# Gated linear attention of an encoder block: gates computed feature-major for two chunks at once, with a scan on VectorE, and element-wise work taken from GpSimd outside the feed-forward

## The chip, the cores and the metric

The kernel runs on one core of a Trainium2 chip. The core's engines each work through their own instructions in order and meet at semaphores: TensorE (PE for matmuls, PEld for loading weights), VectorE (DVE), ScalarE (ACT), GpSimd (POOL), and SyncE (SP), which here issues every DMA. The metric is device time in microseconds (us) for one execution.

## The reference, cut to what matters

One layer, 1024 tokens, width 1024, float32. Each large matrix product is made of three: both operands are split into a rounded high part and a low remainder, and high·high, high·low and low·high are added up.

```python
h = rms_norm(x, norm_mix_g)
proj = h @ w_in              # gla q,k,v,r, gate codes, swa q,k,v, branch gates
# branch A, 4 heads (dk 128, dv 256), forwards and backwards:
z  = lr @ up + bias
lg = maximum(log_sigmoid(z) / 16, -0.5)          # one log gate per token and feature
b  = cumsum(lg, over the tokens of a chunk)
q_dec, k_inv = q * exp(b), k * exp(-b)
scores = where(mask, q_dec @ k_inv.T, 0)
o = scores @ v + q_dec @ state                   # state: decayed from chunk to chunk
y_gla = (rms_norm(o_fwd + o_bwd, out_g) * silu(r)) @ w_o_gla
# branch B: attention in a window of +-128 tokens, QK norm, rotary positions, sinks
y_swa = windowed_attention(...) @ w_o_swa
x = x + (sigmoid(gate_a) * y_gla + sigmoid(gate_b) * y_swa) @ w_out
x = x + (silu(h2 @ w_gate) * (h2 @ w_up)) @ w_ffn_out,   h2 = rms_norm(x, norm_ffn_g)
```

The products of the feed-forward are done with a seven-product scheme on 2x2 blocks, which this change does not touch.

## The kernel before, in words

**Stages.** In order of time: x is loaded and split and the first projections are made (0 to 55 us); linear attention (GLA, 55 to 470 us); windowed attention (SWA, to about 800 us); the two branch projections and the output projection (to 1100 us); the feed-forward.

**Order of the work.** TensorE's order is written by hand. During GLA and SWA the rest of the input projection runs in between: `dense` is a list of generators (`proj_t`, `proj_f`) that give one 512-column matmul at a time, `fill(n)` takes n of them, and `slot(stages, n)` runs the stages of one slot and spreads n dense matmuls between them. `need(key)` takes more of them until a projection is there. The other engines' orders are settled when the program is built, from priorities and estimated readiness, and are fixed from then on.

**GLA.** Chunks of 128 tokens: 4 heads `hd` of 8 chunks `c`, numbered n = 8·hd + c. The table `at` gives each step its slot: `g_gates` in slot n, `g_sums` in n + 1, `g_scores` in n + 2, `g_out` in n + 3. After a head's eight chunks come the backward states and outputs (`g_back_out`) and `g_turn`, which transposes the finished output and writes it to DRAM. A slot carries 40, 31 or 18 dense matmuls (slots 0 to 5, 6 to 34, and the rest).

- `g_gates` (L324) loads q and k feature-major from DRAM (tile `qk`), makes z token-major with one matmul (gate codes `lrS` stationary, `upS` moving), takes Exp, a clamp and Ln, and splits the result into `lh` and `ll`.
- `g_sums` (L345) makes the cumulative sums b on TensorE: two matmuls a direction, `lh` and `ll` against the triangular constant `U`. Out of PSUM come the chunk sums `sm` and exp(b), exp(-b); multiplied by q and k they are the tiles `eb` and `en`, split into `q2` and `kh`, `kl`. Both low parts are made on GpSimd (L366, L368).
- `g_scores` (L370) splits v (`vl` on GpSimd, L379), transposes `en` into `kth`, `ktl` and makes the scores; `g_out` (L398) makes chunk states `pf`, `kb` and outputs `ob`.

**Weight units.** `wunit` (L62) loads 128x512 weights (tile `wr`), rounds them on ScalarE (`wh`) and takes the remainder `wl` on GpSimd (L68), on VectorE only where a call names it. The dense work draws its units through `next_unit`, which keeps up to three ready (AHEAD = 2); one unit feeds 12 (`proj_t`) or 24 (`proj_f`) matmuls.

**SWA.** `k_prep` and `a_prep` normalise and rotate keys and queries; some of the products are on GpSimd (L513 to L516, L537, L538, L557, L577, L579). `k_turn` (L560) transposes the keys. The first two slots carry 60 dense matmuls each, the next ones 46.

**Buffers.** [...] A `mm` tile is free again when ScalarE (`proj_t`, L210) or VectorE (`proj_f`, L146 and L149) has written it to the staging tile `st`.

Of the kernel before, what the change touches and what calls it, by code (L numbers as in the profile page):

```python
# [8 lines left out]
F32 = mybir.dt.float32  # L9
# [20 lines left out]
def body(tc, i, out):  # L30
    nc = tc.nc
    with ExitStack() as root:
# [29 lines left out]
        def wunit(src, n=512, e=None):  # L62
            raw = wp.tile([P, n], F32, tag="wr", name=nm("wr"), bufs=4)
            nc.sync.dma_start(out=raw, in_=src)
            h = wp.tile([P, n], FR, tag="wh", name=nm("wh"), bufs=5)
            nc.scalar.activation(h, raw, AF.Copy)  # L66
            l = wp.tile([P, n], FR, tag="wl", name=nm("wl"), bufs=5)
            (e or nc.gpsimd).tensor_tensor(l, raw, h.bitcast(F32), op=ALU.subtract)  # L68
            return h, l
# [173 lines left out]
        U = gc.tile([P, 2, P], FR, tag="U", name="U")  # L243
# [28 lines left out]
        with tc.manual_schedule(engines={mybir.EngineType.PE}):  # L272
# [28 lines left out]

            Ur = ip.tile([P, 2, P], F32, tag="Ur", name="Ur")
            nc.sync.dma_start(out=Ur, in_=i["c_u"])
            nc.vector.tensor_scalar(U, Ur, -1.0 / 16, None, op0=ALU.mult)
# [19 lines left out]
        def g_gates(hd, c):  # L324

            a = gla[hd, c] = Chunk()
# [3 lines left out]
            a.qk = gtile("qk", (P, 2, P))  # L330
            nc.sync.dma_start(out=a.qk[:, 0], in_=scr[f"q{hd}", s][:, co:co + P])
            nc.sync.dma_start(out=a.qk[:, 1], in_=scr[f"k{hd}", s][:, co:co + P])
            z = chtile((P, 2, P))
            mm(z, lrS[:, c * P:(c + 1) * P], upS[:, :, hd * P:(hd + 1) * P], True, True)
            e = gtile("e", (P, 2, P), bufs=1)
            nc.scalar.activation(e, z, AF.Exp, scale=-1.0)

            nc.vector.tensor_scalar(e, e, float(np.expm1(8.0)), None, op0=ALU.min)
            nc.scalar.activation(e, e, AF.Ln, bias=ones[:, 0:1])
            a.lh = gtile("lh", (P, 2, P), FR)  # L340
            a.ll = gtile("ll", (P, 2, P), FR)
            nc.vector.tensor_copy(a.lh, e)
            nc.vector.tensor_tensor(a.ll, e, a.lh.bitcast(F32), op=ALU.subtract)

        def g_sums(hd, c):  # L345

            a = gla[hd, c]
            bp = chtile((P, 2, 256))
            for d in range(2):
                mm(bp[:, d], a.lh[:, d], U, True, False)  # L350
                mm(bp[:, d], a.ll[:, d], U, False, True)

            a.sm = gtile("sm", (P, 2, 2), bufs=32)
            nc.vector.tensor_copy(a.sm, bp[:, :, 127:129])
            bc = bp.rearrange("p a (c t) -> p (a c) t", c=2)[:, 0:4:3]
            eb = gtile("eb", (P, 2, P), bufs=1)
            a.en = gtile("en", (P, 2, P))
            nc.scalar.activation(eb, bc, AF.Exp)
            nc.scalar.activation(a.en, bc, AF.Exp, scale=-1.0)
            nc.vector.tensor_tensor(eb, eb, a.qk[:, 0:1].to_broadcast([P, 2, P]), op=ALU.mult)  # L360
            nc.vector.tensor_tensor(a.en, a.en, a.qk[:, 1:2].to_broadcast([P, 2, P]), op=ALU.mult)
            a.q2 = gtile(f"q2{c}", (P, 2, 2, P), FR, bufs=2 if c < 5 else 1)
            a.kh = gtile("kh", (P, 2, P), FR)
            a.kl = gtile("kl", (P, 2, P), FR)
            nc.scalar.activation(a.q2[:, :, 0], eb, AF.Copy)
            nc.gpsimd.tensor_tensor(a.q2[:, :, 1], eb, a.q2[:, :, 0].bitcast(F32), op=ALU.subtract)  # L366
            nc.scalar.activation(a.kh, a.en, AF.Copy)
            nc.gpsimd.tensor_tensor(a.kl, a.en, a.kh.bitcast(F32), op=ALU.subtract)  # L368

        def g_scores(hd, c):  # L370
# [8 lines left out]
            nc.gpsimd.tensor_tensor(a.vl, vr, a.vh.bitcast(F32), op=ALU.subtract)  # L379
            kt = chtile((P, 2, P))  # L380
            for d in range(2):
                nc.tensor.transpose(kt[:, d], a.en[:, d], ident)
# [5 lines left out]
            for d in range(2):  # L388
                mm3(sc[:, d], a.kh[:, d], a.kl[:, d], a.q2[:, d, 0], a.q2[:, d, 1], True, True)
# [8 lines left out]
        def g_out(hd, c):  # L398
# [6 lines left out]
            if c:  # L405
                pf = gla[hd, c - 1].pf
                dec = gtile("dec", (P, 1))
                nc.scalar.activation(dec, a.sm[:, 0, 1:2], AF.Exp, bias=gla[hd, c - 1].sm[:, 0, 0:1])
# [12 lines left out]
            if c:  # L421
                mm3(o, a.q2[:, 0, 0], a.q2[:, 0, 1], th, tl, False, True)
# [3 lines left out]
        def g_back(hd, c):  # L426

            a = gla[hd, c]
            if c < NC - 1:
                n = gla[hd, c + 1]  # L430
                dec = gtile("decb", (P, 1))
                nc.scalar.activation(dec, a.sm[:, 1, 0:1], AF.Exp, bias=n.sm[:, 1, 1:2])
# [8 lines left out]
        def g_back_out(hd, c):  # L441
            a = gla[hd, c]
            if c < NC - 1:
                o2 = chtile((P, 256))
                mm3(o2, a.q2[:, 1, 0], a.q2[:, 1, 1], a.thb, a.tlb, True, True)
# [33 lines left out]
        for n in range(NH * NC):  # L479
            hd, c = divmod(n, NC)  # L480
            cb = hd * NC + NC + 3 + (NC - 1 - c)
            tt = cb + c % 2 + (2 if hd == NH - 1 else 1)
            for j, (t, f) in enumerate(((n, g_gates), (n + 1, g_sums), (n + 2, g_scores), (n + 3, g_out),
                                        (cb, g_back_out), (tt, g_turn))):
                at[t, j + (j == 5 and c % 2)] = (f, hd, c)
# [27 lines left out]
        nc.gpsimd.tensor_tensor(qA[:, :, 0:64], cosb, gb_[0], op=ALU.mult)  # L513
        nc.gpsimd.tensor_tensor(qA[:, :, 64:128], cosb, gb_[1], op=ALU.mult)
# [659 lines left out]
```

## Time and profile before

| | before |
|---|---|
| time, median of 3 runs | 1748.46 us (1748.05 to 1749.23) |
| the profiled execution's own time | 1748.99 us |
| its span in the profile | 1747.2 us |
| busy: PE, PEld | 1701.6, 1408.8 us |
| busy: DVE, ACT, POOL | 1105.4, 866.4, 564.4 us |
| granted TensorE clock, mean | 0.993 |

The busy time of an engine is the time in which at least one of its instructions ran. Matmuls overlap in the pipeline: one of 512 columns takes some 400 ns from start to end, while the next one starts after some 230 ns, so how close TensorE is to its limit is read from the distance between starts. "a<-b,c" names the written and the read tiles without their numbers.

### The profile page before, as it was taken

What the parts mean: (1) busy time and instruction counts of PE and PEld (TensorE: products, weight loads), DVE (VectorE), ACT (ScalarE), POOL (GpSimd) and SP (SyncE); (2) the same over time, 40 slices, a digit from 0 to 9 for tenths busy, and PEclk for the clock granted to TensorE, in tenths of its full rate; (3) what the DMA queues carried; (4) which work ended last, traced back from release to release, by engine and by line L of the source; (5) the groups of instructions that cost most, each with busy time, mean ns of one, the idle gap of its engine ahead of it and who ended that gap; (6) DMA issues with size and microseconds to landing.
All of it is one profiled execution on the core that took longest, in us unless ns stands there. A gap on an engine that the chain in (4) does not pass through costs nothing. (4 is left out here: it accounts for less than half of the span.)

```text
span 1747.2 us, 24463 instructions
## 1 busy us (share of the span) xinstructions
PE 1701.6 (97%) x8008; PEld 1408.8 (81%) x8008; DVE 1105.4 (63%) x1998; ACT 866.4 (50%) x2019; POOL 564.4 (32%) x491
## 2 busy tenths in 40 slices
PE   8999999999999999999999999999999999899998
PEld 6788888888778888878878888788888888787776
DVE  6446666664387655536463268877788888789454
ACT  6455766776447656544454456533333333343342
POOL 3444535544353222112455430333343333100000
PEclk9999999999999999999999999999999999999999
DMA  5433343444533232227766645333234434685333
GB/s 193 138 113 103 119 129 120 122 129 138 167 118 118 88 97 91 79 73 246 238 192 187 193 132 181 109 132 127 91 102 146 152 138 140 233 295 170 96 96 103
DMA packets 158496, 246.03 MB, mean 141 GB/s; under 512 B 18111, under 2 KB 47807, under 8 KB 158369
## 3 DMA queue, kind: packets, MB, share of 16 engines
q1 hardware_dynamic: 158368, 244.48, 43.8%
q8 instruction: 63, 1.03, 0.3%
q14 instruction: 65, 0.52, 0.1%
HBM read 177.30 MB, written 67.11 MB: 140 GB/s over the span
## 5 line engine op out<-in xcount | busy, mean ns | idle before, releaser
L68 POOL TENSOR_TENSOR wl<-wr,wh 128x512 fp32r<-128x512 f32 (+1 forms) x226 | 300.3, 1334 | 471.3 <-ACT wh L66 395.3
L66 ACT ACTIVATE wh<-wr 128x512 fp32r<-128x512 f32 (+1 forms) x256 | 158.1, 625 | 133.7 <-PE mm L72 89.6
L72 PE MATMUL mm<-xh,wh 128*128 128x512 f32 x512 | 205.4, 401 | 6.7 <-ACT xh L263 6.7
L72 PE MATMUL mm<-xl,wh 128*128 128x512 f32 x512 | 205.1, 401 | 0.9 <-DVE xl L264 0.9
L72 PE MATMUL mm<-xh,wl 128*128 128x512 f32 x512 | 172.2, 401 | 0.0
L848 POOL TENSOR_TENSOR ws<-wr,wr 128x512 f32<-128x512 f32 x44 | 67.0, 1525 | 231.3 <-DMA wr<-in_w_fi_dram 126.3
L72 PE MATMUL mm<-wh,xh 128*128 128x512 f32 x320 | 127.0, 397 | 2.6 <-ACT st L210 1.3
L72 PE MATMUL mm<-wh,xl 128*128 128x512 f32 x320 | 126.8, 396 | 0.0
L72 PE MATMUL mm<-wl,xh 128*128 128x512 f32 x320 | 126.3, 395 | 0.0
L72 PEld LDWEIGHTS mm<-xh,wh 128*128 128x128 f32 x512 | 98.0, 191 | 23.3 <-ACT xh L263 6.7
L72 PEld LDWEIGHTS mm<-xl,wh 128*128 128x128 f32 x512 | 97.9, 191 | 18.7 <-DVE xl L264 1.9
L72 PEld LDWEIGHTS mm<-xh,wl 128*128 128x128 f32 x512 | 96.0, 191 | 16.7
L829 ACT ACTIVATE wh<-ws 128x512 fp32r<-128x512 f32 x88 | 55.4, 629 | 98.7 <-PE ch L856 41.5
L829 ACT ACTIVATE wh<-a 128x512 fp32r<-128x512 f32 x66 | 41.7, 632 | 103.2 <-PE mm L992 58.0
L830 DVE TENSOR_TENSOR wl<-ws,wh 128x512 fp32r<-128x512 f32 x88 | 76.4, 875 | 13.5 <-ACT wh L829 13.5
L992 PE MATMUL mm<-hl,wh 128*128 128x512 f32 x176 | 70.7, 402 | 11.0 <-DVE hl L967 11.0
L830 DVE TENSOR_TENSOR wl<-a,wh 128x512 fp32r<-128x512 f32 x66 | 45.5, 691 | 55.1 <-ACT wh L829 55.0
L829 ACT ACTIVATE wh<-wr 128x512 fp32r<-128x512 f32 x52 | 32.9, 632 | 77.9 <-PE ch L856 39.3
L72 PEld LDWEIGHTS mm<-wh,xh 128*128 128x128 f32 x320 | 60.3, 188 | 13.9 <-ACT st L210 2.0
L992 PE MATMUL mm<-hh,wh 128*128 128x512 f32 x176 | 70.0, 398 | 1.2 <-ACT hh L966 1.2
L992 PE MATMUL mm<-hh,wl 128*128 128x512 f32 x176 | 70.1, 398 | 0.0
L72 PEld LDWEIGHTS mm<-wh,xl 128*128 128x128 f32 x320 | 60.3, 188 | 10.0
(502 smaller groups left out, 4785.9 us busy)
## 6 DMA issues: line engine op xcount, KB each, us to landing
wr<-in_w_fi_dram SPq DMA_DIRECT2D x102, 256.0 KB, 2.8
wr<-in_w_t_dram SPq DMA_DIRECT2D x80, 256.0 KB, 2.7
wr<-in_w_f_dram SPq DMA_DIRECT2D x64, 256.0 KB, 2.8
B<-c SPq DMA_DIRECT2D x44, 256.0 KB, 2.1
T<-tx SPq DMA_DIRECT2D x44, 256.0 KB, 2.2
a<-in_w_fo_dram SPq DMA_DIRECT2D x44, 256.0 KB, 4.9
hr<-T SPq DMA_DIRECT2D x44, 256.0 KB, 2.7
hr<-B SPq DMA_DIRECT2D x33, 256.0 KB, 4.0
```

The costliest lines, as they stand in the source:

```text
L66: nc.scalar.activation(h, raw, AF.Copy)
L68: (e or nc.gpsimd).tensor_tensor(l, raw, h.bitcast(F32), op=ALU.subtract)
L72: nc.tensor.matmul(o, a, b, start=start, stop=stop)
L829: nc.scalar.activation(h, src, AF.Copy)
L830: nc.vector.tensor_tensor(l, src, h.bitcast(F32), op=ALU.subtract)
L848: e.tensor_tensor(t, x, y, op=op)
L992: nc.tensor.matmul(ys[m], a[:, c], b, start=f0, stop=f1, skip_group_check=True)
```

## The change: what it does

- **Gates for a pair of chunks, feature-major.** `g_gates` runs for even c only and covers c and c + 1. z is made with `upS` stationary and 256 tokens of `lrS` moving, so features lie on the partitions. The cumulative sum over tokens is a `tensor_tensor_scan` on VectorE (with `mask`, which is 0 at each chunk's first token and 1 elsewhere), so the two matmuls a direction against `U`, the constant `U` and its load, the split into `lh` and `ll`, and the step `g_sums` are gone. Sums, exponentials and products with q and k are done on VectorE and ScalarE on tiles twice as wide. `q2` is kept per pair, as `q2f` (two buffers) and `q2b`.
- **Slots.** Gates of a pair stand in slot n of its even chunk and come first in the slot; `g_scores` and `g_out` stay at n + 2 and n + 3. The turn stands at cb + c % 2 + 2 for all heads (before, + 1 for the first three). Slot 1 now holds no step, and therefore no dense matmul.
- **GpSimd.** All element-wise work before the feed-forward is on VectorE: the `wl` of every weight unit, `vl`, `kl`, the low parts of `q2`, and the products of SWA. GpSimd keeps its part of the feed-forward.

```diff
-        def wunit(src, n=512, e=None):
+        def wunit(src, n=512):
...
-            (e or nc.gpsimd).tensor_tensor(l, raw, h.bitcast(F32), op=ALU.subtract)
+            nc.vector.tensor_tensor(l, raw, h.bitcast(F32), op=ALU.subtract)
...
-        U = gc.tile([P, 2, P], FR, tag="U", name="U")
+        mask = gc.tile([P, 4, P], F32, tag="mask", name="mask")
+        nc.vector.memset(mask, 1.0)
+        nc.vector.memset(mask[:, :, 0:1], 0.0)
...
-            mm(z, lrS[:, c * P:(c + 1) * P], upS[:, :, hd * P:(hd + 1) * P], True, True)
-            e = gtile("e", (P, 2, P), bufs=1)
-            nc.scalar.activation(e, z, AF.Exp, scale=-1.0)
-            nc.vector.tensor_scalar(e, e, float(np.expm1(8.0)), None, op0=ALU.min)
-            nc.scalar.activation(e, e, AF.Ln, bias=ones[:, 0:1])
...
-            nc.vector.tensor_copy(a.lh, e)
-            nc.vector.tensor_tensor(a.ll, e, a.lh.bitcast(F32), op=ALU.subtract)
-        def g_sums(hd, c):
-            a = gla[hd, c]
-            bp = chtile((P, 2, 256))
             for d in range(2):
-                mm(bp[:, d], a.lh[:, d], U, True, False)
-                mm(bp[:, d], a.ll[:, d], U, False, True)
...
+                mm(z[:, d], upS[:, d, hd * P:(hd + 1) * P], lrS[:, c * P:(c + 2) * P], True, True)
+            e = gtile("e", (P, 2, 2, P), bufs=1)
+            ef = e.rearrange("p d j t -> p (d j t)")
+            nc.scalar.activation(ef, z.rearrange("p d t -> p (d t)"), AF.Exp, scale=-1.0)
+            nc.vector.tensor_scalar(ef, ef, float(np.expm1(8.0)), None, op0=ALU.min)
+            nc.scalar.activation(ef, ef, AF.Ln, bias=ones[:, 0:1])
...
+            nc.vector.tensor_tensor_scan(csf, mask.rearrange("p c t -> p (c t)"), ef, 0.0, op0=ALU.mult, op1=ALU.add)
...
+            nc.vector.tensor_tensor(e[:, 0], cs[:, 0], cs[:, 0, :, 63:64].to_broadcast([P, 2, P]), op=ALU.subtract)
...
+            nc.scalar.activation(csf, ef, AF.Exp, scale=-1.0 / 16)
+            nc.scalar.activation(ef, ef, AF.Exp, scale=1.0 / 16)
+            pr.en = gtile("en", (P, 2, 256))
+            nc.vector.tensor_tensor(pr.en[:, 0], x2[:, 0], qk[:, 1], op=ALU.mult)
...
+            pr.q2 = (gtile("q2f", (P, 2, 256), FR), gtile(f"q2b{c}", (P, 2, 256), FR, bufs=(3, 2, 2, 1)[c // 2]))
...
-            nc.gpsimd.tensor_tensor(a.vl, vr, a.vh.bitcast(F32), op=ALU.subtract)
+            nc.vector.tensor_tensor(a.vl, vr, a.vh.bitcast(F32), op=ALU.subtract)
...
-            tt = cb + c % 2 + (2 if hd == NH - 1 else 1)
+            tt = cb + c % 2 + 2
...
-                slot([(lambda v=at[t, j]: v[0](*v[1:])) if (t, j) in at else None for j in (6, 5, 4, 3, 2, 1, 0)], n)
+                slot([(lambda v=at[t, j]: v[0](*v[1:])) if (t, j) in at else None for j in (0, 5, 4, 3, 2, 1)], n)
...
-            nc.gpsimd.tensor_tensor(b[:, :, 0:64], qn[:, :, 64:128], s, op=ALU.mult)
-            nc.gpsimd.tensor_tensor(b[:, :, 64:128], qn[:, :, 0:64], s, op=ALU.mult)
+            nc.vector.tensor_tensor(b[:, :, 0:64], qn[:, :, 64:128], s, op=ALU.mult)
+            nc.vector.tensor_tensor(b[:, :, 64:128], qn[:, :, 0:64], s, op=ALU.mult)
```

Three places show how instructions move. On TensorE in the third head, before, between dense matmuls (`mm`), the cumulative sums of one chunk (`U`) and the z of the next one:

```order
L72 MATMUL mm_3057<-xh_99,wl_2941 128x512
L72 MATMUL ch_3204<-U,lh_3100 128x256
L72 MATMUL ch_3204<-U,ll_3101 128x256
L72 MATMUL ch_3204<-U,lh_3100 128x256
L72 MATMUL ch_3204<-U,ll_3101 128x256
L72 MATMUL mm_3056<-xh_100,wh_2939 128x512
```

The same place now, the z of a pair at the head of its slot, with a turn (`ident`, `ob`) behind it:

```order
L72 MATMUL mm_3095<-wh_3226,xl_114 128x512
L72 MATMUL ch_3349<-lrS,upS 128x256 x2
L72 MATMUL mm_3092<-wh_3259,xh_100 128x512
L72 MATMUL mm_3092<-wl_3261,xh_100 128x512
L72 MATMUL mm_3092<-wh_3259,xl_116 128x512
L72 MATMUL mm_3093<-wh_3259,xh_100 128x512
L72 MATMUL mm_3093<-wl_3261,xh_100 128x512
L474 MATMUL ch_3392<-ident,ob_700_2918 128x128 x2
```

The four matmuls against `U` are gone for every chunk; a pair has two z matmuls where two chunks had one each. On VectorE in the same head, the gates of one chunk before (with a backward output, `ob`, in between):

```order
L354 COPY sm_2747<-ch_2742 128x4
L360 TENSOR_TENSOR eb_2749<-eb_2749,qk_2592 128x256
L361 TENSOR_TENSOR en_2750<-en_2750,qk_2592 128x256
L338 TENSOR_SCALAR e_2771<-e_2771 128x256
L342 CAST lh_2775<-e_2771 128x256
L446 TENSOR_TENSOR ob_248_1203<-ob_248_1203,ch_2788 128x256
L343 TENSOR_TENSOR ll_2776<-e_2771,lh_2775 128x256
```

and of a pair now, from its scan (`mask`) on, with a weight unit's `wl` and steps of other chunks in between:

```order
L348 SCALAR_TENSOR_TENSOR cs_3356<-mask,e_3352 128x512
L351 TENSOR_SCALAR sm_3358<-cs_3356 128x8
L354 TENSOR_TENSOR e_3352<-cs_3356 128x256
L352 TENSOR_TENSOR sm_3358<-sm_3358 128x4
L355 TENSOR_TENSOR e_3352<-cs_3356 128x2x127
L357 TENSOR_SCALAR e_3352<-cs_3356 128x2
L68 TENSOR_TENSOR wl_3566<-wr_3562,wh_3564 128x512
L455 TENSOR_TENSOR ob_568_2431<-ob_568_2431,ch_3428 128x256
L365 TENSOR_TENSOR en_3366<-cs_3356,qk_3346 128x256
L366 TENSOR_TENSOR cs_3356<-cs_3356,qk_3346 128x256
```

The scan is listed as a SCALAR_TENSOR_TENSOR; `wl` has come over from GpSimd. At the start of SWA, VectorE before, from the first table `qB` to the rotated first key `qn` (GpSimd made the rest of the tables and `sq`):

```order
L515 SCALAR_TENSOR_TENSOR qB<-sinb,qg 128x8x64
L96 TENSOR_SCALAR rt_6306<-ss_6299 128x2
L97 TENSOR_TENSOR rt_6306<-rt_6306,rl_6303 128x2
L98 SCALAR_TENSOR_TENSOR rt_6306<-rt_6306,rl_6303 128x2
L99 SCALAR_TENSOR_TENSOR rs_6302<-rt_6306,rl_6303 128x2
L532 SCALAR_TENSOR_TENSOR qn_6311<-kvr_6294,rs_6302,kg 128x128 x2
```

and now the first rows of the same stretch:

```order
L523 TENSOR_TENSOR qA<-cosb,qg 128x8x64
L524 TENSOR_TENSOR qA<-cosb,qg 128x8x64
L525 SCALAR_TENSOR_TENSOR qB<-sinb,qg 128x8x64
L526 TENSOR_TENSOR qB<-sinb,qg 128x8x64
L567 TENSOR_TENSOR vSl_5731<-kvr_5763,vSh_5723 128x256
L591 TENSOR_TENSOR qn_5981<-qr_5964,qA 128x512
L96 TENSOR_SCALAR rt_5775<-ss_5768 128x2
```

Four instructions that ran on GpSimd, and the first query's product, now stand ahead of the key's own chain on VectorE.

More of the change, by code (lines that the diff above doesn't have):

```diff
@@ L324, in g_gates @@
         def g_gates(hd, c):
-            a = gla[hd, c] = Chunk()
+            pr = Chunk()
+            for j in range(2):
+                a = gla[hd, c + j] = Chunk()
+                a.pr, a.j, a.t = pr, j, slice(j * P, (j + 1) * P)
             s, co = c // 4, (c % 4) * P
@@ new lines, in g_gates @@
+            nc.vector.tensor_tensor(x2[:, 1], x2[:, 1], qk[:, 0], op=ALU.mult)
+            pr.kh = gtile("kh", (P, 2, 256), FR)
+            pr.kl = gtile("kl", (P, 2, 256), FR)
+            nc.scalar.activation(pr.kh, pr.en, AF.Copy)
+            nc.vector.tensor_tensor(pr.kl, pr.en, pr.kh.bitcast(F32), op=ALU.subtract)
+            pr.q2 = (gtile("q2f", (P, 2, 256), FR), gtile(f"q2b{c}", (P, 2, 256), FR, bufs=(3, 2, 2, 1)[c // 2]))
+            for q2, x in zip(pr.q2, (x1[:, 0], x2[:, 1])):
+                nc.scalar.activation(q2[:, 0], x, AF.Copy)
+                nc.vector.tensor_tensor(q2[:, 1], x, q2[:, 0].bitcast(F32), op=ALU.subtract)
@@ L481, in body @@
             cb = hd * NC + NC + 3 + (NC - 1 - c)
-            tt = cb + c % 2 + (2 if hd == NH - 1 else 1)
-            for j, (t, f) in enumerate(((n, g_gates), (n + 1, g_sums), (n + 2, g_scores), (n + 3, g_out),
+            tt = cb + c % 2 + 2
+            for j, (t, f) in enumerate(((n, g_gates), (n + 2, g_scores), (n + 3, g_out),
                                         (cb, g_back_out), (tt, g_turn))):
-                at[t, j + (j == 5 and c % 2)] = (f, hd, c)
+                if j or c % 2 == 0:
+                    at[t, j + (j == 4 and c % 2)] = (f, hd, c)
                 last = max(last, t)
@@ L895, in p11 @@
             if f < NB:
-                w = wunit(i["w_fi"][f, 0], e=nc.vector)
+                w = wunit(i["w_fi"][f, 0])
             else:
```

79 lines of the change are left out of this document (34 added, 45 removed).

## The prediction

> **What bounds the kernel now.** I read the page's busy times first, then how far apart TensorE's matmuls start, then the stretches in which the change works, then TensorE's waits there.
>
> ```profile
> PE 1701.6 (97%) x8008; PEld 1408.8 (81%) x8008; DVE 1105.4 (63%) x1998; ACT 866.4 (50%) x2019; POOL 564.4 (32%) x491
> ```
>
> TensorE stands out, but overlapped matmuls can look busy without being at their limit. The timeline of TensorE in the middle of GLA (columns: start, duration, both in us) settles it:
>
> ```profile
> 307.74 0.39 PE L72 MATMUL mm<-wh,xl 128*128 128x512 f32 x1
> 307.96 0.28 PE L72 MATMUL ch<-U,lh 128*128 128x256 f32 x1
> 308.08 0.28 PE L72 MATMUL ch<-U,ll 128*128 128x256 f32 x1
> 308.20 0.28 PE L72 MATMUL ch<-U,lh 128*128 128x256 f32 x1
> 308.32 0.28 PE L72 MATMUL ch<-U,ll 128*128 128x256 f32 x1
> 308.44 0.39 PE L72 MATMUL mm<-wh,xh 128*128 128x512 f32 x1
> 308.67 0.39 PE L72 MATMUL mm<-wl,xh 128*128 128x512 f32 x1
> ```
>
> A 512-column matmul takes a place of 0.23 us in the stream, a 256-column one 0.12 us, and nothing stands between them: here TensorE is the bound, and a matmul that goes gives back its place. By stages (columns: the stretch, its length, then busy us and instructions of PE, PEld, DVE, ACT, POOL, the granted clock, DMA):
>
> ```profile
> core 0: us, PE busy (x) PEld busy (x) DVE busy (x) ACT busy (x) POOL busy (x), PEclk, DMA share, GB/s
> 130.00:410.00 280.00, 276.72 (x1563) 237.67 (x1562) 181.43 (x421) 190.16 (x565) 136.47 (x139) 1.00 0.40 121
> 489.00:585.00 96.00, 96.00 (x465) 80.22 (x464) 72.67 (x213) 56.87 (x203) 37.84 (x48) 0.98 0.37 116
> ```
>
> The first is most of GLA, the second the part of SWA in which keys and queries are both prepared. TensorE hardly pauses in either, at full clock. All that TensorE waits for from 55 to 489 us is this (total us, times, longest):
>
> ```profile
> PE ch L563 <- ACT rl L94: 3.8, 1, 3.8
> PE ch L72 <- ACT kb L415: 1.4, 1, 1.4
> PE ch L465 <- ACT ob L459: 1.4, 1, 1.4
> PE mm L72 <- ACT st L210: 1.3, 1, 1.3
> PE mm L72 <- DVE st L149: 0.6, 1, 0.6
> ```
>
> That is 8.5 us in 434. So the change can win what it takes from TensorE's stream and part of these waits, and can lose what VectorE, which gets GpSimd's work, now makes TensorE wait.
>
> **TensorE: the sums go.** The instructions that read the constant U:
>
> ```profile
> L72 PE MATMUL ch<-U,lh x64: 277/281/386, 65.0 to 405.5; 128*128 128x256 f32 x64
> L72 PE MATMUL ch<-U,ll x64: 277/283/287, 65.1 to 405.7; 128*128 128x256 f32 x64
> ```
>
> 128 matmuls at a place of (308.44 - 307.96)/4 = 0.12 us are **15.4 us**. The z matmuls stay 32 of 256 columns, so cost the same. Slot 1's 40 dense matmuls are not saved: they run later, in the flush at SWA's end.
>
> **VectorE: can it carry the rest?** What GpSimd does in the GLA stretch, and what one of each costs on either engine (min/median/max ns):
>
> ```profile
> L68 POOL TENSOR_TENSOR wl<-wr,wh 128x512 fp32r<-128x512 f32 x60 | 78.7, 1314 | 68.7 <-ACT wh L66 29.3 <-issue 27.6 <-PE mm L72 4.2
> L368 POOL TENSOR_TENSOR kl<-en,kh 128x256 fp32r<-128x256 f32 x26 | 20.7, 796 | 3.3 <-ACT kh L367 3.3
> L366 POOL TENSOR_TENSOR q<-eb,q 128x256 fp32r<-128x256 f32 x27 | 20.2, 747 | 50.3 <-ACT q L365 50.3
> L379 POOL TENSOR_TENSOR vl<-vr,vh 128x256 fp32r<-128x256 f32 x26 | 20.1, 772 | 26.8 <-ACT vh L378 9.5 <-DMA o<-ot 3.7 <-PE mm L72 3.5
> ...
> L68 POOL TENSOR_TENSOR wl<-wr,wh x226: 1017/1295/2074, 4.5 to 1032.8; 128x512 fp32r<-128x512 f32 x112, 128x384 fp32r<-128x384 f32 x1
> L68 DVE TENSOR_TENSOR wl<-wr,wh x30: 673/684/1199, 1033.4 to 1204.4; 128x512 fp32r<-128x512 f32 x30
> L343 DVE TENSOR_TENSOR ll<-e,lh x32: 424/426/1558, 59.1 to 400.2; 128x256 fp32r<-128x256 f32 x32
> L98 DVE SCALAR_TENSOR_TENSOR rt<-rt,rl x45: 148/163/1674, 42.6 to 1102.8; 128x2 f32<-128x2 f32 x24, 128x4 f32<-128x4 f32 x16, 128x512 f32<-128x512 f32 x4, 128x8 f32<-128x8 f32 x1
> ```
>
> Moved onto VectorE: 60 x 0.684 + 79 x 0.426 = 74.7 us. The gates themselves nearly balance: for a pair go ten 256-wide instructions and two small ones (4.6 us at 0.426 and 0.16), and come two 512-wide, clamp and scan (1.4; the third, kl, is counted with the moved ones), six 256-wide (2.6) and three small (0.5), 4.5 us, if the scan costs what another 512-wide instruction does. No row shows a scan. From below it is bounded by 0.68; from above I take GpSimd's 1.30, the slowest two-input row of this size; the nearest row is 0.68 and I use it, with 13 x 0.6 = 8 us of VectorE time kept for the range. VectorE's demand is thus at most 181.4 + 74.7 = 256 us, or 264, against 280 less 26 chunks x 0.48 = 267.5 us of TensorE: 96 to 99%. But 181.4 holds time that goes: L343's median is 426 ns and its maximum 1558, and its slow ones fall where GpSimd works. In this stretch alone:
>
> ```profile
> L343 DVE TENSOR_TENSOR ll<-e,lh 128x256 fp32r<-128x256 f32 x26 | 16.2, 622 | 0.6
> ```
>
> 622 less 426 is 0.2 us of stretching on each. If half of the 421 instructions carry as much, 42 us go when GpSimd is silent, and VectorE stands at about 214 us of 267, 80%. I take this, and keep 99% for the range.
>
> [...]
>
> **Does a pair's chain arrive in time?** It is longer than before: exponential, clamp, logarithm, scan, subtractions, two exponentials, four products, roundings, remainders. ScalarE's part is five 512-wide and two 256-wide instructions, priced by
>
> ```profile
> L66 ACT ACTIVATE wh<-wr 128x512 fp32r<-128x512 f32 (+1 forms) x256 | 158.1, 625 | 133.7 <-PE mm L72 89.6
> ```
>
> at no more than 7 x 0.63 = 4.4 us; VectorE's is 3 x 0.68 + 8 x 0.43 + 3 x 0.16 = 6 us: 10.4 us and the handoffs. The scores of a pair's first chunk come at the end of the second slot after: 62 dense matmuls x 0.23 = 14 us and more with the chunks' own matmuls. For the first pair, with slot 1 empty, it is 60 x 0.23 = 14 us alone. So it fits, with over 3 us for handoffs in the worst place. A wait that is new: `q2f` has two buffers, and a pair's is read last in slot n + 4, where the pair after next starts. ScalarE's write of it may wait there for `g_out`, with `kth` and `wh` queued behind it; 1 us each time would still lie within the three weight units held ready.
>
> **The start of SWA.** The 3.8 us wait is this (starts and durations again):
>
> ```profile
> 483.70 0.39 PE L72 MATMUL mm<-xh,wl 128*128 128x512 f32 x1
> 487.94 0.66 PE L563 MATMUL ch<-ident,qn 128*128 128x128 f32 x2 [3.85 <-ACT rl L94]
> ...
> 484.24 1.25 POOL L68 TENSOR_TENSOR wl<-wr,wh 128x512 fp32r<-128x512 f32 x1
> ...
> 484.30 1.34 DVE L539 TENSOR_TENSOR qn<-qn,cosb 128x128 f32<-128x128 f32 x1 [0.77 <-POOL sq L538]
> 487.03 0.81 DVE L542 TENSOR_TENSOR qn<-qn,sq 128x128 f32<-128x128 f32 x1
> ...
> L541 DVE TENSOR_TENSOR qn<-qn,sq x8: 277/280/809, 486.3 to 575.6; 128x128 f32<-128x128 f32 x8
> ```
>
> TensorE waits for the first rotated key, made on VectorE while GpSimd runs; ScalarE is named only because it was last to signal. Its four last steps took from 484.30 to 487.84, 3.5 us, where 4 x 0.28 = 1.1 would do without stretching: 2.4 us. The small steps ahead of it gain up to 1 us each, but the new order puts qA twice, half of qB, a remainder and a query's product ahead on VectorE, 4 x 0.68 + 0.43 = 3.1 us, of which GpSimd's part ran beside it before. I let these two cancel: **2.4 us** won; from below nothing, from above all 3.8.
>
> In the SWA stretch VectorE takes over 48 GpSimd instructions, the first and one of the others being
>
> ```profile
> L68 POOL TENSOR_TENSOR wl<-wr,wh 128x512 fp32r<-128x512 f32 x13 | 16.8, 1294 | 27.1 <-ACT wh L66 25.3 <-PE mm L72 1.7
> L577 POOL TENSOR_TENSOR sq<-qr,qB 128x256 f32<-128x256 f32 x7 | 5.2, 748 | 4.3 <-issue 3.8 <-ACT sq L521 0.5
> ```
>
> so 13 x 0.684 + 35 x 0.426 = 23.8 us at most on top of 72.7: 96.5 of 96 us, less 0.2 x 213/2 = 21 us of stretching, 78%. This is the tightest place. From 800 to 1100 us VectorE has `wl` of 12 matmuls (2.7 us of TensorE) for 0.68 us: covered.
>
> **What VectorE's queue costs.** VectorE and ScalarE wait for each other in order, and what a fuller queue delays is TensorE's PSUM: 1.4 and 1.3 us of the waits above came from ScalarE held up by VectorE, as in
>
> ```profile
> 381.56 0.91 ACT L459 ACTIVATE ob<-ob,ors 128x256 f32<-128x256 f32 x2 [0.86 <-DVE ors L99]
> ```
>
> Those can go with the stretching, and others can come. From below I bound the balance at -2.7 us, both gone; from above at +20, worked out in the second rival; I take +2, near the waits that the trace has now. **Sum:** 1748.99 - 15.4 - 2.4 + 2.0 = 1733.2 us for an execution like the profiled one (span 1747.2 and 1.8 around it), which lies 0.5 above the median of the runs: **1733 us**.
>
> **Rivals.**
> - *Stretching held back more than I count* (0.12). All five waits above go but the last `ob` one, and TensorE's small pauses in the branch stage, where `wl` came from GpSimd: -15.4 - 7.1 and some -3, 1723 us. For it: each has GpSimd or VectorE in its chain. Against it: VectorE is fuller.
> - *VectorE becomes the bound* (0.12), the one on the slower side. Place: GLA's slots and SWA's first eight. VectorE's longest waits for ScalarE in the GLA stretch are
>
> ```profile
> DVE tl L412 <- ACT th L411: 25.0, 20, 2.7
> DVE e L338 <- ACT e L336: 13.7, 16, 1.3
> DVE ktl L386 <- ACT kth L385: 12.3, 13, 2.6
> ```
>
>   51 us. If the stretching does not go (264) and half of them stays (25), VectorE needs 289 us where TensorE needs 267: 22 us lost, and in SWA 96.5 + 8 against 96, 8 more: 1749 - 15 + 30 = 1764 us. It decides from the point at which demand and waits pass TensorE's 267 by the 15 us won, 282.
> - *The places that come free are filled with waits* (0.08): TensorE issues less and pauses more, for scores whose pair comes late or `mm` banks that VectorE empties late, some 1 us a pair over 16 pairs: 1748 us. [...]
>
> **How the numbers follow.** The forecast, 0.68, runs from 1727 (waits gone) to 1743 (VectorE's balance at +12). With the faster rival and most of the same one the range is **1723 to 1748**, which leaves out the slower rival and a little of each tail. About 0.2%, 3.5 us, is what a measurement of this kernel can tell from no change: faster 0.68 + 0.12 = 0.80, same 0.08, slower 0.12.
>
> **What would show it.** Right: no matmul on U, TensorE's span from the first z to the first key turn shorter by about 15 us, L541's like near 0.28 us at SWA's start, the wait of the first `ident,qn` matmul under 2 us, VectorE at 80 to 85% in GLA. Wrong: TensorE waits for `wl`, `kl`, `q2f` or `st` adding up to over 10 us between 55 and 620 us, a scan far over 1.3 us, or VectorE without pauses while TensorE has them.

## The result, and the profile after

| | before | after |
|---|---|---|
| time, median of 4 runs | 1748.85 us (1748.05 to 1749.83) | 1724.73 us (1722.66 to 1725.41) |
| ratio after to before | | 0.986, 95% interval 0.9843 to 0.9877 |
| the profiled execution: time, span | 1748.99, 1747.2 us | 1724.57, 1722.5 us |

The change saves 24.1 us; 15.8 was forecast. The page's busy times after:

```profile
PE 1683.8 (98%) x7880; PEld 1391.1 (81%) x7880; DVE 1183.8 (69%) x2348; ACT 867.3 (50%) x1939; POOL 151.8 (9%) x110
```

TensorE has 128 matmuls less. GpSimd lost 564.4 - 151.8 = 412.6 us of work, and VectorE, which took it over, grew by only 1183.8 - 1105.4 = 78.4 us. The same two stretches of the program as in the prediction (columns: the stretch, its length, then busy us and instructions of PE, PEld, DVE, ACT, POOL, the granted clock, DMA share and GB/s):

```profile
130.00:380.00 250.00, 249.28 (x1386) 213.50 (x1384) 186.50 (x503) 178.30 (x478) 0.00 (x0) 1.00 0.43 131
461.00:555.00 94.00, 93.47 (x460) 77.93 (x459) 71.79 (x258) 58.23 (x203) 0.00 (x0) 1.00 0.37 117
```

TensorE still hardly pauses; VectorE stands at 186.5/250 = 75% in GLA and 71.8/94 = 76% in SWA. What TensorE waits for from 55 to 462 us (total us, times, longest):

```profile
PE ch L474 <- ACT ob L468: 1.6, 1, 1.6
PE mm L72 <- DVE st L149: 0.7, 1, 0.7
PE ch L573 <- issue: 0.3, 1, 0.3
PE ch L72 <- ACT vh L385: 0.3, 1, 0.3
PE ch L72 <- DVE sl L404: 0.3, 1, 0.3
```

That is 3.2 us, against the 8.5 us of the prediction's table. The large one, at the first key, has shrunk from 3.85 to 0.32 us; its chain in the timeline (start, duration):

```profile
457.39 0.28 DVE L547 TENSOR_TENSOR sq<-qn,sinb 128x128 f32<-128x128 f32 x1
457.59 0.29 DVE L548 TENSOR_TENSOR sq<-qn,sinb 128x128 f32<-128x128 f32 x1
...
458.39 0.29 DVE L551 TENSOR_TENSOR qn<-qn,sq 128x128 f32<-128x128 f32 x1
...
458.78 0.41 PE L573 MATMUL ch<-ident,qn 128*128 128x128 f32 x2 [0.32 <-issue]
```

Six steps of 0.28 or 0.29 us follow each other every 0.2 us. Before, single steps there took 1.34 and 0.81 us.

**Where the time went.** I took the distances between consecutive matmul starts in the two traces. A *pause* is what a distance over 0.45 us has above the usual 0.23 us. Pauses: 43.4 us before, 35.1 after, -8.3. The distances behind the 128 `U` matmuls: 7.7 + 7.7 = 15.4 us, gone. Everything else together: -1.0; in it, matmuls at half clock lose less (about 8.2 us before and 4.6 after, an estimate from the distances), and other distances grew. The sum, -24.7, is the difference of the two spans. The rest of this document asks which part of the change took the 8.3 us away.

### The profile page after: what moved, and what is told of

It is laid out like the page before. It is cut to its first block, busy times and chain, and to the rows that moved or that the text cites. A ratio compares the mean times of both kernels' runs of the same rounds, so it can differ in the third digit from the quotient of the medians.

```text
span 1722.5 us, 23762 instructions
## 1 busy us (share of the span) xinstructions
PE 1683.8 (98%) x7880; PEld 1391.1 (81%) x7880; DVE 1183.8 (69%) x2348; ACT 867.3 (50%) x1939; POOL 151.8 (9%) x110
## 5 line engine op out<-in xcount | busy, mean ns | idle before, releaser
L68 DVE TENSOR_TENSOR wl<-wr,wh 128x512 fp32r<-128x512 f32 (+1 forms) x256 | 176.0, 691 | 94.6 <-ACT wh L66 90.0
L72 PEld LDWEIGHTS mm<-xh,wh 128*128 128x128 f32 x512 | 97.0, 189 | 23.4 <-ACT xh L266 6.6
L72 PEld LDWEIGHTS mm<-xh,wl 128*128 128x128 f32 x512 | 95.2, 190 | 16.6
L840 DVE TENSOR_TENSOR wl<-ws,wh 128x512 fp32r<-128x512 f32 x88 | 76.5, 877 | 13.5 <-ACT wh L839 13.5
L1002 PE MATMUL mm<-hl,wh 128*128 128x512 f32 x176 | 71.1, 404 | 10.8 <-DVE hl L977 10.8
L630 ACT ACTIVATE p<-p,nm,rs 128x384 f32<-128x384 f32 (+1 forms) x64 | 42.9, 674 | 56.1 <-DVE nm L624 56.1
```

The lines of the kernel that those rows point to most:

```text
L68: nc.vector.tensor_tensor(l, raw, h.bitcast(F32), op=ALU.subtract)
L72: nc.tensor.matmul(o, a, b, start=start, stop=stop)
L630: nc.scalar.activation(p[:, h, :w], p[:, h, :w], AF.Exp, bias=nm_[:, h:h + 1], scale=a.rs[:, h:h + 1], accum_out=dn[:, h:h + 1])
L840: nc.vector.tensor_tensor(l, src, h.bitcast(F32), op=ALU.subtract)
L1002: nc.tensor.matmul(ys[m], a[:, c], b, start=f0, stop=f1, skip_group_check=True)
```

## The experiments

Each ratio is to the kernel before, run beside it on the same chip. Pauses are counted as above.

| kernel | median us | ratio (95%) | pauses us |
|---|---|---|---|
| the changed kernel | 1724.73 | 0.986 (0.9843 to 0.9877) | 35.1 |
| e1_gates_alone | 1768.33 | 1.0105 (1.0081 to 1.0129) | 61.3 |
| e2_engine_alone | 1734.84 | 0.9919 (0.9904 to 0.9933) | 32.5 |
| e3_z_five_times | 1739.87 | 0.9943 (0.9928 to 0.9958) | 36.0 |
| e4_fill_first_slot | 1751.18 | 1.002 (1.0011 to 1.003) | 40.5 |
| e5_swa_on_gpsimd | 1733.45 | 0.9909 (0.9884 to 0.9935) | 40.4 |
| e6_wl_on_gpsimd | 1739.45 | 0.9949 (0.9934 to 0.9965) | 46.2 |
| e7_turn_as_before | 1723.05 | 0.9857 (0.984 to 0.9874) | 34.0 |
| e8_scan_thrice | 1740.42 | 0.9953 (0.9935 to 0.9971) | 43.5 |
| e9_gates_alone_last_in_slot | 1744.02 | 0.998 (0.9965 to 0.9995) | 50.7 |
| e10_gates_last_in_slot | 1727.24 | 0.9882 (0.9867 to 0.9897) | 38.1 |
| e11_ffn_on_vector | 1715.46 | 0.9814 (0.9799 to 0.9829) | 26.5 |
| e12_idle_gpsimd | 1748.10 | 0.9996 (0.9987 to 1.0005) | 49.8 |

The kernel before, beside which they ran, had medians of 1748.77 (e1 to e4), 1747.04 (e5, e6, e8, e9) and 1748.77 us (e7, e10 to e12). So a difference of medians from two of these groups can be off by nearly 2 us; the ratios take this out.

### The two halves of the change, each alone

e1, from the kernel after (the same for `kl`, the low part of `q2`, `vl` and the products of SWA):

```diff
-            nc.vector.tensor_tensor(l, raw, h.bitcast(F32), op=ALU.subtract)
+            (e or nc.gpsimd).tensor_tensor(l, raw, h.bitcast(F32), op=ALU.subtract)
```

> The changed kernel with every product and low part ahead of the feed-forward put back on GpSimd, so the gates by scan and the later turn stand alone. Theory A (three terms: the U matmuls give 15.4 us wherever they stood; the waits at 484 and 772 us and the stretches at half clock behind them belong to GpSimd and come back): 1733 us, 1730 to 1736, the first head's turn waits over 3 us again, with a granted clock near 0.5 for some us behind it. Rival B (the U matmuls and the freed score order give all 24 us): 1724 to 1727. Rival C (the scan on VectorE, beside a GpSimd that slows it again, runs late): 1740 or more, with waits on kb, st or q2 in the linear attention.

e2, from the kernel before, with the same edit the other way round at all these places:

```diff
-            (e or nc.gpsimd).tensor_tensor(l, raw, h.bitcast(F32), op=ALU.subtract)
+            (e or nc.vector).tensor_tensor(l, raw, h.bitcast(F32), op=ALU.subtract)
```

> The kernel before with only the GpSimd work ahead of the feed-forward moved to VectorE, U matmuls kept. Theory A (what the change gives besides the U matmuls, 24.1 - 15.4 = 8.7 us, comes from the engine): 1740 us, 1737 to 1743, first head's turn wait under 1 us, no granted clock under 0.9 at 486 or 776 us. Rival B (VectorE becomes the bound with the separate gates and the split of e): 1749 or more. Rival C (the engine gives nothing): 1747 to 1750.

Theories A and B for e1 fell. C had the sign, and of the waits that it named only `st` came at any size (2.6 and 1.9 us, before 0.6 and 1.3); the largest are others. The gates by themselves make the kernel 1% **slower**, although the 15.4 us of `U` matmuls are gone. The engine by itself gives 13.9 us, more than the 8.7 expected. From 55 to 475 us the largest waits of TensorE in e1 are for things that it did not wait for before:

```profile
PE ch L72 <- DVE sh L403: 5.1, 9, 1.1
PE ch L72 <- ACT kth L392: 2.8, 4, 1.7
PE ch L72 <- DVE sl L404: 2.7, 5, 0.8
```

In e2, from 55 to 800 us, hardly anything is left of the waits before the change:

```profile
PE ch L637 <- ACT p L626: 2.7, 7, 1.6
PE ch L465 <- ACT ob L459: 1.4, 1, 1.4
```

Kernel e9 is e1 with the gates last in the slot, as before the change, and e10 is the kernel after with the same edit:

```diff
-  ... for j in (0, 5, 4, 3, 2, 1)], n)
+  ... for j in (5, 4, 3, 2, 1, 0)], n)
```

> The kernel of e1_gates_alone with the gates taken last in their slot, as before the change, in place of first. Theory A (gates first puts a pair's scan, its 512-wide passes and its low parts ahead of the slot's score chain on VectorE, ScalarE and GpSimd, and the slow GpSimd makes that late: the waits on sh, kth and sl, 10.6 us): 1748 to 1758. Rival B (the order does nothing; VectorE is stretched by GpSimd whatever stands first): 1764 or more.

> The changed kernel, all on VectorE, with the gates taken last in their slot. With GpSimd in the loop this order was worth 24 us (1768 against 1744). Theory A (the order counts only where a slow GpSimd makes a pair's burst long; with VectorE the waits left between 60 and 440 us are under 4 us in all): 1721 to 1726. Rival B (the burst at the head of the slot still holds the score chain up, as three scans in place of one did, which cost 15 us ahead of the first turn): 1718 or less. Rival C (gates last come too late for their scores): 1728 or more, with waits on kh, kl or q2.

Together the medians make a table of two choices:

| gates | GpSimd ahead of the feed-forward | all on VectorE |
|---|---|---|
| old | 1748.85 | 1734.84 |
| by scan, last in the slot | 1744.02 | 1727.24 |
| by scan, first in the slot | 1768.33 | 1724.73 |

The halves do not add up. Gates put first cost 24 us where GpSimd makes the low parts (1768.33 - 1744.02; 22 by the ratios). Where VectorE makes them, no cost can be told from nothing: the intervals of e10 and of the kernel after overlap. e9 came out faster than either of its theories allowed, and e10 fell between its theories A and C.

In e9 the three waits above, 10.6 us, are gone, and the pauses are 10.6 us less. That is under half of the 24. Some 5 us more are matmuls at half clock: between 55 and 475 us they lose about 5.3 us in e1 and 0.7 in e9, an estimate from the distances between their starts. The rest are mostly distances that grew and stay under 0.45 us. All this fits a pair's burst of gates, with slow low parts in it, that stands ahead of the scores of the same slot. That it is the burst is argued from the order and from these waits; no run times it by itself.

### What a TensorE place is worth

e3:

```diff
             for d in range(2):
-                mm(z[:, d], upS[:, d, hd * P:(hd + 1) * P], lrS[:, c * P:(c + 2) * P], True, True)
+                for _ in range(5):
+                    mm(z[:, d], upS[:, d, hd * P:(hd + 1) * P], lrS[:, c * P:(c + 2) * P], True, True)
```

> The changed kernel with each of its z products computed five times into the same tile: 32 x 4 = 128 more matmuls of 256 columns, the number and width of the U matmuls that went. Theory A (a TensorE matmul there costs its 0.12 us, for TensorE sets the end in this stretch): 1724.7 + 15.4 = 1740 us, 1737 to 1743. Rival B (they hide in waits): under 1732.

1739.87 - 1724.73 = 15.1 us for 128 matmuls, 0.118 us each, with pauses within 0.9 us of the kernel after. TensorE's stream sets the end here, and a place in it has its full price (theory A).

### Is it GpSimd's results that come late, or GpSimd itself?

e6 moves only the weights' low parts back (in `wunit`, the edit shown for e1).

> The changed kernel with only the weights' low parts (wl, ahead of the feed-forward) back on GpSimd. The gates alone came to 1768 us, 43 us over the changed kernel. Theory A (it is GpSimd's load beside VectorE that stretches VectorE's instructions, and wl is 69 of the 118 us of GpSimd between 150 and 400 us): more than half of the 43 us, 1746 or more, with waits on sh, kth and sl in the linear attention. Rival B (it is the low parts in the score chain, kl, q2 and vl, that come late behind wl in GpSimd's queue; wl by itself costs little): under 1735.

14.7 us slower, between the two theories: a third of e1's 43 us. The stretch of GLA in e6:

```profile
130.00:380.00 250.00, 244.71 (x1337) 206.91 (x1337) 181.36 (x436) 167.97 (x457) 71.12 (x54) 1.00 0.40 121
```

VectorE issued 67 instructions less than after (436 against 503) and was busy for only 5.1 us less, while GpSimd worked 71.1 us. TensorE got through fewer matmuls there, 1337 against 1386, so the stretch holds a little less work for everyone. VectorE got next to nothing for what it gave away. e12 leaves all of VectorE's work in place and adds GpSimd work that serves nothing:

```diff
+            for x in range(6):
+                nc.gpsimd.tensor_tensor(idle, mask[:, 2:4, :].rearrange("p c t -> p (c t)"),
+                                        mask[:, 0:2, :].rearrange("p c t -> p (c t)") if x else a.vh.bitcast(F32),
+                                        op=ALU.mult)
             a.sh = gtile("sh", (P, P), FR)
```

> The changed kernel with six GpSimd products of 128x256 for each chunk of the linear attention, into a tile that nobody reads: 192 of some 0.76 us, 146 us of GpSimd beside VectorE (e1_gates_alone had 118 us of it between 150 and 400). The first of the six reads the chunk's vh so that they keep pace; no instruction waits for them but the next write of vh two chunks later. Theory A (GpSimd stretches VectorE's instructions by being busy beside it, and this alone costs time): 1732 or more, VectorE's vl over 500 ns and L343 near 800 in the mean against 421 and 427. Rival B (what costs is that TensorE's operands wait for GpSimd's results; the stretch alone stays hidden): 1724 to 1728.

The same stretch of GLA:

```profile
130.00:380.00 250.00, 237.95 (x1278) 200.25 (x1277) 213.36 (x466) 158.46 (x426) 114.32 (x134) 0.99 0.38 118
```

23.4 us slower, nearly the whole gain of the change: theory A. In its trace VectorE, ScalarE and TensorE run the same instructions in the same order as in the kernel after. Only one instruction waited for the new ones, a `vh` of ScalarE, for 3.9 us; the rest is not waiting for GpSimd's results. The groups of VectorE between 150 and 400 us, first of the kernel after, then of e12 (busy us, mean ns of one | idle before):

```profile
L393 DVE TENSOR_TENSOR ktl<-ch,kth 128x256 fp32r<-128x256 f32 x24 | 10.1, 422 | 7.5 <-ACT kth L392 7.5
L386 DVE TENSOR_TENSOR vl<-vr,vh 128x256 fp32r<-128x256 f32 x23 | 9.7, 421 | 1.2 <-ACT vh L385 1.1
L404 DVE TENSOR_TENSOR sl<-sp,sh 128x128 fp32r<-128x128 f32 x24 | 7.0, 291 | 0.6
L343 DVE TENSOR_SCALAR e<-e 128x512 f32<-128x512 f32 x11 | 4.7, 427 | 6.3 <-ACT e L341 6.3
```

```profile
L409 DVE TENSOR_TENSOR sl<-sp,sh 128x128 fp32r<-128x128 f32 x24 | 15.7, 654 | 0.6
L387 DVE TENSOR_TENSOR vl<-vr,vh 128x256 fp32r<-128x256 f32 x23 | 13.5, 587 | 0.6 <-ACT vh L386 0.6
L394 DVE TENSOR_TENSOR ktl<-ch,kth 128x256 fp32r<-128x256 f32 x23 | 9.6, 416 | 3.6 <-ACT kth L393 3.6
L344 DVE TENSOR_SCALAR e<-e 128x512 f32<-128x512 f32 x11 | 6.3, 577 | 0.3 <-ACT e L342 0.3
```

`sl` and `vl`, both inputs in SBUF, go from 291 to 654 ns and from 421 to 587. `ktl`, which reads one input from PSUM (`ch`), stays at its 0.42 us. The clamp of `e`, with one SBUF input, is stretched too, 427 to 577 (near 800 was expected). Of the other rows of the same stretch, those that read a PSUM tile stay as well (`ob<-ob,ch` 415 and 412 ns, `pf<-pf,dec,ch` 477 and 473); of those that read SBUF alone, `tl` goes from 484 to 693, and the subtraction `e<-cs` stays at 418. So no row with a PSUM input is stretched here, and most of the others are; what in the engines makes it so is not shown.

Starts and ends in the traces show the stretching instruction by instruction. In e12, 23 of the 32 `sl` start while a GpSimd instruction runs: they take 502 to 850 ns, the other nine 276 to 294. Of the 32 `ktl`, 21 start beside a running GpSimd instruction and take 410 to 426 ns, the others 411 to 424. It was so before the change already: 12 of the 32 `ll` (L343) start while GpSimd runs and take 629 to 1558 ns, and the other 20 take 424 to 428, among them five beside which a GpSimd instruction starts later.

e11 takes the same idea to the feed-forward, which the change had left on GpSimd:

```diff
-            s1 = comb(nc.gpsimd, F.r21, F.r22, ALU.add)
+            s1 = comb(nc.vector, F.r21, F.r22, ALU.add)
...
-            nc.gpsimd.tensor_tensor(p5, p5, p1, op=ALU.add)
+            nc.vector.tensor_tensor(p5, p5, p1, op=ALU.add)
...
-            s3 = comb(nc.gpsimd, F.r11, F.r21, ALU.subtract)
+            s3 = comb(nc.vector, F.r11, F.r21, ALU.subtract)
...
-            nc.gpsimd.tensor_tensor(u2, u2, r1, op=ALU.mult)
+            nc.vector.tensor_tensor(u2, u2, r1, op=ALU.mult)
```

(and the same in `gate0`).

> The changed kernel with the feed-forward's GpSimd work on VectorE too. There VectorE is busy 336.5 of 430 us and GpSimd 151.6 us in 106 instructions of 128x512, which take VectorE 0.69 us each as wl does: 73 us more, 409 of 430 or 95%. Theory A (VectorE becomes the bound there or nearly so, as nothing of it can wait): 1728 to 1745, with waits on u, c and ws in the feed-forward. Rival B (VectorE's instructions there shrink by more than they gain, as in the linear attention): 1715 to 1722.

**1715.46 us, the fastest kernel of this study**: rival B, where theory A expected a loss. The same 420 us of feed-forward, first of the kernel after, then of e11:

```profile
1060.00:1480.00 420.00, 414.53 (x1815) 339.43 (x1814) 332.81 (x427) 150.36 (x252) 149.04 (x104) 1.00 0.39 128
```

```profile
1060.00:1480.00 420.00, 418.98 (x1847) 346.26 (x1845) 333.43 (x538) 154.07 (x256) 0.00 (x0) 1.00 0.40 132
```

VectorE carries 111 instructions more in the same busy time, 333 us. I had added 73 us to a busy time that already held the stretching. Some of its instructions over the whole run (min/median/max ns), again after and e11:

```profile
L840 DVE TENSOR_TENSOR wl<-ws,wh x88: 674/682/1786, 1073.4 to 1475.0; 128x512 fp32r<-128x512 f32 x88
L858 DVE TENSOR_TENSOR ws<-ws,wr x22: 682/1762/1772, 1072.2 to 1452.1; 128x512 f32<-128x512 f32 x22
```

```profile
L840 DVE TENSOR_TENSOR wl<-ws,wh x88: 680/684/694, 1073.5 to 1467.4; 128x512 fp32r<-128x512 f32 x88
L858 DVE TENSOR_TENSOR ws<-ws,wr x22: 678/692/695, 1071.6 to 1443.5; 128x512 f32<-128x512 f32 x22
```

The durations are not spread out but stand in groups. Of the 22 `ws`, the 17 that start while a GpSimd instruction runs take 1755 to 1772 ns, and the other five 682 to 693. Of the 88 `wl`, 66 start with no GpSimd instruction running and take 674 to 693 ns; of the other 22, one takes 687 ns, 14 take 1358 to 1376 and seven 1775 to 1786. With GpSimd silent the maximum of these rows is 695 ns.

### The start of SWA: a wait, and a clock

e5 puts only the products of SWA back on GpSimd (qA, half of qB, the rotary products, the low part of v), as they were before.

> The changed kernel with only the windowed attention's products (table, rotary, low part of v) back on GpSimd; the linear attention and the weight splits stay on VectorE. Theory A (the first head's turn wait of 3.8 us, the 2.4 us ahead of the last probabilities and the half-clock stretches behind them come from these products): 1724.7 + 3.5 + 2.4 + 2 to 3 = 1732 us, 1729 to 1735. Rival B (they came from the weight splits' low parts on GpSimd, which stand in the same queue): 1724 to 1727, turn wait under 1.5 us.

8.7 us slower, as theory A said, and two waits of TensorE return between 455 and 800 us:

```profile
PE ch L647 <- ACT p L636: 3.8, 17, 0.7
PE ch L573 <- issue: 3.5, 1, 3.5
```

After the result I also had a theory on the clock. Before the change, TensorE alone behind the wait of 3.85 us reads so (the stretch, its length, busy us and instructions of PE, granted clock, DMA):

```profile
484.00:488.00 4.00, 0.15 (x2) 0.76 0.45 134
488.00:491.00 3.00, 3.00 (x9) 0.50 0.57 153
491.00:494.00 3.00, 3.00 (x11) 0.68 0.07 23
```

9 matmuls fall into the 3 us at half clock, and 16 into the same 3 us in e4. Were such stretches a hidden part of the price of a wait? e4, from the kernel before, takes the wait away by itself:

```diff
-  ... 60 if t < 2 else 46 if t < 2 * KT + 2 else 28)
+  ... 84 if t < 1 else 60 if t < 2 else 46 if t < 2 * KT + 2 else 28)
```

> The kernel before with 84 in place of 60 dense matmuls in the first slot of the windowed attention, so that TensorE has work while the first head is made ready; the matmuls are only taken earlier, none is added. Theory A (the wait of 3.85 us goes, and with it the 6.83 us at half clock behind it, worth some 2.5 to 3.4 us): 1742 to 1744. Rival B (the half clock costs nothing beside the wait): 1745 to 1746. Rival C (the dense matmuls are missing later and the wait comes there): 1748 or more.

In e4 the wait is gone and so is the half clock behind it:

```profile
488.00:491.00 3.00, 3.00 (x16) 1.00 0.52 154
```

yet the time is not better than before (ratio 1.002): rival C. TensorE's one remaining wait in SWA tells why; before the change, and in e4:

```profile
PE ch L637 <- ACT p L626: 3.3, 7, 2.2
```

```profile
PE ch L637 <- ACT p L626: 5.9, 21, 1.6
```

The wait moved to the probabilities, where the matmuls used to fill the first slot were missing, or the chain behind the first key was still as long; which of the two, e4 does not tell. By the matmul starts, pauses fell by 2.9 us and the distances behind the dense 512-column matmuls, which are 0.43 us at half clock (488.8 to 490.1 us, before) for 0.23, by 2.3, but the turns of the probabilities took 3.9 more, the feed-forward 1.2 more, and the first matmul came 1.3 later, the last two for reasons of their own. In the changed kernel that same wait is smaller than before,

```profile
PE ch L647 <- ACT p L636: 1.9, 11, 0.2
```

so the change shortened the chain where e4 only covered its start. The clock theory as I had it fell: the half clock is real, but its 2 us were not won by filling. It is part of the price of waits elsewhere: by the distances behind matmuls that start at half clock, between 55 and 475 us it takes about 5 us in e1, 4 in e8 and 3 in e12 (estimates), and nothing in the kernel after, where the granted clock is 1.00 in that stretch.

### Room on VectorE, and the turn

e8 issues the scan three times.

```diff
-            nc.vector.tensor_tensor_scan(csf, mask.rearrange("p c t -> p (c t)"), ef, 0.0, op0=ALU.mult, op1=ALU.add)
+            for _ in range(3):
+                nc.vector.tensor_tensor_scan(csf, mask.rearrange("p c t -> p (c t)"), ef, 0.0, op0=ALU.mult, op1=ALU.add)
```

> The changed kernel with its scan issued three times into the same tile: 16 x 2 x 1.22 = 39 us more of VectorE in the linear attention, which takes it from 75% to some 88% there, and 2.45 us more in the chain from z to the scores. Theory A (VectorE has room, and the chain has two slots): 1723 to 1728. Rival B (VectorE is near to the bound already): 1732 or more, with waits on VectorE's tiles in the linear attention.

15.7 us slower for 39 us of added VectorE work, so rival B. But 14.4 of the 16.6 us that its trace loses between the first and the last z are lost ahead of the first turn, at 191 us in the kernel after: with bursts 2.45 us longer, what TensorE waits for between 55 and 210 us begins

```profile
PE mm L72 <- DVE st L149: 2.9, 1, 2.9
PE mm L72 <- ACT st L210: 2.2, 1, 2.2
PE ch L72 <- DVE sh L404: 1.9, 2, 1.3
```

These are PSUM tiles (the kernel has four `mm` and four `ch` ones) emptied late and scores made late, behind a pair's burst on VectorE. VectorE was not full there, nor in GLA as a whole (third column of busy times):

```profile
53.00:210.00 157.00, 147.97 (x736) 122.97 (x735) 113.45 (x254) 83.11 (x196) 0.00 (x0) 0.97 0.37 117
130.00:380.00 250.00, 245.18 (x1330) 207.82 (x1329) 203.36 (x505) 164.85 (x444) 0.00 (x0) 0.99 0.40 122
```

It is 72% and 81% busy. So how long the queue was held counted here before how full it was. How much of the 15.7 us the longer bursts alone cost is not shown: the half clock is in it (granted clock 0.97 from 53 to 210 us), and VectorE and ScalarE also run some of their other instructions in another order than in the kernel after.

e7:

```diff
-            tt = cb + c % 2 + 2
+            tt = cb + c % 2 + (2 if hd == NH - 1 else 1)
```

> The changed kernel with the turn of a head's outputs one slot earlier for the heads but the last, as before the change. Theory A (the turn had waited nowhere in the linear attention but at its very end, and the last head's slot is the same in both): 1724 to 1726, ratio to before 0.985 to 0.988, no new wait on ob. Rival B (the later turn keeps the turns off the queues' bursts of a pair's gates): 1728 or more, with waits on ob or ors between 190 and 440 us.

No difference: 0.9857 and 0.986, each well inside the other's interval. The later turn is neither gain nor loss.

## Why the prediction was right, and where it was not

The change is faster and the time lies in the range, but at its lower end: 1724.73 us is under the forecast's own 1727 to 1743 and inside the range by the faster rival's share. Two errors of opposite sign, below, cancelled in part, and that was luck.

- **The `U` matmuls, -15.4: right.** They are gone, 7.7 + 7.7 us of starts with them, and e3 brings back 15.1 for the same number. But the gates as a whole are worth only 1734.84 - 1724.73 = 10.1 us with VectorE. With GpSimd, put first as in the change, they are a loss, and put last they gain 3 us (1747.04 - 1744.02). With VectorE, pauses are 2.6 us more than in e2 (`st`, `vh`, `sl`), and the other distances 1.2 more.
- **The first key, -2.4: the mechanism right, the size low.** The wait fell by 3.5 us and the steps took the 0.28 us that I named. I had let the products newly ahead of it cancel the gain of the small steps; they did not.
- **What VectorE's queue costs, +2: this is the step that failed.** Its sign was wrong. e2, which is that step with the first key, came to -13.9, where I had -2.4 + 2.0 = -0.4. I used the stretching by GpSimd only to lower VectorE's demand, and then priced the queue from the few waits of GLA, as if GpSimd's leaving could at best return 2.7 us there. e12 shows the price directly: GpSimd's presence in GLA, serving nothing, costs 23 us with the order of all engines' work unchanged. How e2's 13.9 us split between that and results of GpSimd that came late is not shown. So the engine gave 13.5 us more than forecast, and the gates 5.3 less (10.1 for 15.4): 8.2 us, and the forecast missed by 24.1 - 15.8 = 8.3.
- **VectorE at 80% in GLA, 78% in SWA:** 75% and 76%, so the sign of 80 to 85% did not come. More stretching went than the half that I counted: 75% of the 267 us is 200, 14 under the 214 forecast, though 13 scans took 7 us more than priced.
- **The scan at 0.68 us: wrong.** By the trace

```profile
L348 DVE TENSOR_TENSOR_SCAN cs<-mask,e x16: 1220/1225/1226, 56.2 to 353.7; 128x512 f32<-128x512 f32 x16
```

  it takes 1.22, close to the upper bound and 0.54 us more than the 0.68 of the row that I priced it by. Whether this cost time was not measured: e8 says that 2.45 us more a pair do.
- **The faster rival, 1723 us, is where the time landed,** for some of its reasons: the waits on `kb` (1.4), on ScalarE's `st` (1.3) and on the first key went; VectorE's `st` stayed (0.6, now 0.7), and `ob` rose from 1.4 to 1.6. The branch stage, where I put 3 us on `wl`, is 2.4 us shorter by its first matmuls (796.6 to 1058.6 us, before 821.8 to 1086.2). Before the change its pauses do stand ahead of matmuls that read `wl`, and TensorE's waits from 780 to 1062 us are

```profile
PE mm L72 <- POOL wl L68: 1.0, 2, 0.6
```

  But the stage is just as short in e6, whose `wl` is on GpSimd too, so that alone does not make them; what else it takes stays open. SWA behind the first key gave 2.4 us that the rival did not have (28 dense matmuls that now run there taken off), and the start, up to the first z, 2.2; the feed-forward took 2.9 back.
- **First z to first key turn, shorter by about 15: it is 26.9** (432.2 us before, 405.2 after). I had left out of this sign what I said of slot 1: 28 dense matmuls fewer stand in that stretch now (1333 for 1361), 6.4 us at 0.23, and the shorter waits are in it too.
- **The slower rival:** I let it decide at a demand of 282 us against TensorE's 267. e8 and e12 lose 16 and 23 us with VectorE busy 203 and 213 of 250 us in GLA (rows above), 81% and 85%. Arriving late began here well ahead of being full, so the point was set too high.
- **Costed at nothing, and nothing:** the later turn (e7), the gates first in the slot with VectorE (e10). Costed at nothing in every place and not so with GpSimd: the same order, 24 us (e1 against e9).

## What to carry to other kernels

Before work is given to GpSimd to relieve VectorE, compare the minimum and the median of VectorE's two-input SBUF instructions in the trace: where they have a large value beside GpSimd's work and a small one elsewhere (here 1762 and 682 ns for `ws`), VectorE's busy time already holds GpSimd's time, and taking the work back can be free, as 111 more instructions in the same 333 us were. Price a queue by how long a burst in it holds up what stands behind, not by its mean load. When a change has two halves, time each alone: here one of them, as it stands in the change, is a loss without the other.

## What the runs showed of the hardware that I had not expected

- GpSimd's 149 us in the feed-forward were worth less than nothing: without it, at the same VectorE busy time, the kernel is 1724.73 - 1715.46 = 9.3 us faster. Ahead of the feed-forward the same move, with all else as before, gave 13.9 us (e2).
- TensorE's granted clock fell to 0.50 behind some of its waits, in pieces of 3.41 or 6.83 us, and once more at the kernel's end: before, at 42.4, 486.1, 776.2 us and in the feed-forward; after, in the feed-forward alone, with a new one at 1558.1 us. The waits at 486.1 and 776.2 us were of 3.85 and 2.21 us. In the feed-forward one of 2.56 us, before, has no such piece behind it (its end at 1583.5 us), and one of 2.49, after, has the new one.
